# Rotation tables by one transpose of a narrow tile and row-repeating loads from a DRAM scratch, in a hybrid attention and gMLP block

## The chip, the cores and the metric

One core of a Trainium2 chip runs the whole kernel. The metric is the device time of one execution in microseconds (us), and a time given for a kernel is the median of several executions. The profile is of one execution; its span runs from the first instruction to the last.

Engines: PE is TensorE (matmuls and transposes by matmul), PEld its weight loads, DVE VectorE, ACT ScalarE, POOL GpSimd, and SP the engine whose queue issues most of this kernel's DMAs. PSUM is the memory into which PE accumulates; SBUF holds everything else on the chip; DRAM is the memory off the engines.

## The reference

One layer on a sequence of 1024 positions of width 1024, in float32. A root-mean-square norm is followed by one wide projection whose columns are queries, keys, values, gates and the inputs of a gMLP branch. What concerns the change is the rotation of the first 16 of the 64 dimensions of each query and key head:

```python
def partial_rope(x, pos):
    half = ROPE_DIM // 2          # 8
    inv_freq = ROPE_THETA ** (-(jnp.arange(half, dtype=jnp.float32) * 2.0) / ROPE_DIM)
    ang = pos.astype(jnp.float32)[:, None] * inv_freq[None, :]
    cos = jnp.cos(ang)[None, :, None, :]
    sin = jnp.sin(ang)[None, :, None, :]
    ...
    out = jnp.concatenate([x1 * cos - x2 * sin, x2 * cos + x1 * sin, rest], axis=-1)
```

The rotated queries and keys go into windowed attention with sinks (16 query heads, 2 key heads). Its output and the gMLP's are gated, projected, added to the residual and normed once more. The tables of cosines and sines depend on the position and on 8 frequencies alone, and are the same for all heads.

## The kernel before, in words

**Matmuls.** Every projection is a product of 1024x1024 blocks. `gemm_pair` takes two blocks of 128 output features (a pair, named by its first block m = 0, 2, 4, 6) and computes them by seven products instead of eight (b11, t1, t2, b21, t3, b22, t4, in this order), on sums and differences of quarters. A product (`product`, the matmul of L362) is 12 matmuls of 128x512: 4 steps of the inner dimension, each as high part by high part, high by low, and low by high. The high and low parts of a weight tile `wr` or of a sum of weight tiles `s` are `wh` (cast on ACT, L176) and `wl` (subtraction on DVE, L177).

**Around a pair.** Behind each product a hook is called; further work is put in there piece by piece, by generators that go on at each call. While a pair runs, the weight parts of the next one are made: its two tiles `wr` (four DMAs of 128 KB each for a query pair, L212, on SP) are loaded a pair earlier still, DVE forms their sums (L262 to L265), ACT and DVE split them. After t3, DVE subtracts the accumulator from x22 (L397); t4 accumulates into that same bank of PSUM, so t4 has to wait for L397. After b21, L392 adds to x11, and after b22, L401 to x12.

**Order.** Tiles have a fixed number of buffers per tag (`wr` 3, `wh` and `wl` 3 each, `rot` 5, `qhl` 3). A scheduler sets the order of each engine's instructions from the dependencies and its own estimate of durations; the engines then run their streams in that order, each instruction waiting for its semaphores. A DMA that waits at the head of SP's queue holds all behind it. SP's DMAs use eight semaphores in turn, so the ninth also waits for the first to have landed.

**The change's place.** The stage computes the queries, pairs m = 0, 2, 4, 6, through `gemm_pair(hb, finish, part_of_q)`. Each finished quarter goes to DRAM unrotated (`q_raw`, L520) and split into high and low parts (`q_hl`, L1241, from tiles `qhl` made by L1233 and L1236). At m = 2 the generator `rope_tables` makes two tables `tab`, of cosines and of sines, each 128x512: partition 64a + 8h + d holds frequency d for half a of the positions, the same for the eight h, and the 512 columns are the positions of that half. At m = 4 the generators `rotate_keys` and `rotate` begin: they load the rows to be rotated (`rot<-k_raw` L1254, `rot<-q_raw` L1290), multiply by the tables on DVE (L1271 to L1280 for the keys, L1310 to L1317 for the queries) and write the result over its place in `k_dr` and `q_hl`. A further `rotate` follows in the next pair, the first of `z` (destination `z_dr`), whose results only the second half of attention needs. The next pair after that begins attention: its score matmuls (L1438) read tiles `k` and `q` that SP loads from `k_dr` and `q_hl` (L1353, L1385).

**How the tables are made before.** The host passes cosines and sines as 128 x (8 tiles of positions x 16). Both are loaded into one tile. For each table DVE copies it, four times 128x128 (L1214), into a `wide` tile in which the frequencies stand eight times; PE transposes the four pieces (L1221) into a bank of tag `tp`; ACT copies the bank to `tab` (L1222).

## Time and profile before

| | |
|---|---|
| time, median of 3 runs | 897.91 us (896.01 to 897.95) |
| span of the profiled execution | 895.1 us |
| PE busy | 883.5 us, 99% of the span |
| DVE, ACT, POOL busy | 685.0, 580.7, 152.2 us |
| granted TensorE clock, mean | 0.998 |
| place of `rope_tables` in the span | 228 us (load of the tables) to 240 us (last copy to `tab`) |

The timed runs stand 0.9 to 2.9 us above the span of the profiled execution: the page counts only from the first instruction to the last. A busy PE is one in which matmuls follow each other; a matmul's own duration overlaps that of the next, so that a step between two starts (about 0.227 us in a product here) is what one costs, not its duration of 0.39 us.

### The profile page before, as it was taken

The numbers are of one execution on the slowest core, as the hardware profiler recorded it, in microseconds if no ns is written. First come the engines' busy times: TensorE is split into PE (matmuls) and PEld (weight loads), VectorE is DVE, ScalarE is ACT, GpSimd is POOL, SyncE is SP. The second block draws the span as 40 slices with busy tenths as digits, with TensorE's granted clock in tenths as the row PEclk, the third lists the DMA queues.
The fourth block names the chain that finished last, engine by engine and source line by source line (L and its number), as shares of the span: only waits on it lengthen the run. The fifth ranks groups of instructions, "written<-read, shape, count | busy, mean of one in ns | idle before, by whom it ended". The sixth has DMA issues, their size and how long they took to land.

```text
span 895.1 us, 13162 instructions
## 1 busy us (share of the span) xinstructions
PE 883.5 (99%) x4117; PEld 730.8 (82%) x4117; DVE 685.0 (77%) x1362; ACT 580.7 (65%) x1189; POOL 152.2 (17%) x218
## 2 busy tenths in 40 slices
PE   9999999999999999999999999999999999999997
PEld 6888888888888888888888888887888888888886
DVE  7879966566686778888878888846796588479886
ACT  6875523334445489999989999964685375467443
POOL 3322222203030011111211011101121121110012
PEclk9999999999999999999999999999999999999999
DMA  9998888858778767887776689989899789998523
GB/s 333 216 280 207 270 202 172 172 159 266 245 247 299 205 186 188 210 196 192 179 234 216 228 225 229 243 297 336 313 286 385 284 227 255 307 294 283 189 105 131
DMA packets 130962, 212.40 MB, mean 237 GB/s; under 512 B 12778, under 2 KB 59370, under 8 KB 130892
## 3 DMA queue, kind: packets, MB, share of 16 engines
q1 hardware_dynamic: 108280, 148.36, 49.9%
q0 software_dynamic: 22464, 62.93, 31.4%
q8 instruction: 33, 0.54, 0.2%
q14 instruction: 37, 0.30, 0.1%
q10 hardware_dynamic: 148, 0.27, 0.1%
HBM read 146.37 MB, written 86.11 MB: 260 GB/s over the span
## 4 chain that ended last, share of the span: by engine, by line
PE 90%; issue 3%; ACT 3%; DMA 2%; DVE 1%; SPq 0%; POOL 0%; ACTq 0%; POOLq 0%
PE ps_mm L362 39%; PE ps_o L362 25%; PE ps_tp L362 6%; PE ps_sc L362 3%; PE ps_o L793 3%; PE ps_tp L793 2%; PE ps_mm L793 2%; PE ps_sc L1438 2%; PE ps_tp L1511 2%; PE ps_tp L1109 2%; PE ps_o L1546 2%; PE ps_sc L793 1%; DMA a_dr<-x 1%; DMA wr<-in_x_dram 1%; PE ps_sc L663 1%
## 5 line engine op out<-in xcount | busy, mean ns | idle before, releaser
L176 ACT CAST wh<-s 128x1024 fp32r<-128x1024 f32 (+1 forms) x79 | 79.4, 1007 | 75.9 <-PE ps_mm L362 27.6
L177 DVE TENSOR_TENSOR wl<-wr,wh 128x512 fp32r<-128x512 f32 (+1 forms) x77 | 72.1, 938 | 60.0 <-ACT wh L176 59.1
L177 DVE TENSOR_TENSOR wl<-s,wh 128x1024 fp32r<-128x1024 f32 (+1 forms) x79 | 92.6, 1173 | 9.7 <-ACT wh L176 9.5
L176 ACT CAST wh<-wr 128x512 fp32r<-128x512 f32 (+1 forms) x77 | 63.0, 819 | 54.6 <-PE ps_mm L362 31.6
L362 PE MATMUL ps_o<-T_t1h,wh 128*128 128x512 f32 x148 | 57.8, 391 | 0.0
L362 PE MATMUL ps_o<-T_t1h,wl 128*128 128x512 f32 x148 | 57.7, 390 | 0.0
L362 PE MATMUL ps_o<-T_t1l,wh 128*128 128x512 f32 x148 | 57.6, 389 | 0.0
L362 PE MATMUL ps_mm<-T_t3h,wh 128*128 128x512 f32 x140 | 55.0, 393 | 2.0 <-ACT x L387 2.0
L1444 ACT COPY sl<-ps_sc 128x384 f32<-128x384 f32 (+2 forms) x128 | 51.8, 456 | 7.0 <-DVE sm L1450 7.0
L1466 ACT ACTIVATE pr<-pr,sm 128x192 f32<-128x192 f32 (+2 forms) x128 | 56.2, 443 | 0.1
L1450 DVE CUSTOM_DVE_ANT_0 pr<-sl,nsink_sb 128x192 f32<-128x192 f32 (+2 forms) x128 | 48.1, 400 | 10.0 <-ACT sl L1444 8.9
L362 PE MATMUL ps_mm<-T_b11h,wh 128*128 128x512 f32 x140 | 55.0, 393 | 0.0
L362 PE MATMUL ps_mm<-T_b11l,wh 128*128 128x512 f32 x140 | 54.6, 390 | 0.0
L362 PE MATMUL ps_mm<-T_t3h,wl 128*128 128x512 f32 x140 | 54.6, 390 | 0.0
L362 PE MATMUL ps_mm<-T_b11h,wl 128*128 128x512 f32 x140 | 54.6, 390 | 0.0
L362 PE MATMUL ps_mm<-T_t2l,wh 128*128 128x512 f32 x140 | 54.6, 390 | 0.0
L362 PE MATMUL ps_mm<-T_t3l,wh 128*128 128x512 f32 x140 | 54.6, 390 | 0.0
L362 PE MATMUL ps_mm<-T_t2h,wh 128*128 128x512 f32 x140 | 54.6, 390 | 0.0
L362 PE MATMUL ps_mm<-T_t2h,wl 128*128 128x512 f32 x140 | 54.5, 389 | 0.0
L362 PE MATMUL ps_mm<-T_t4h,wh 128*128 128x512 f32 x136 | 53.4, 393 | 0.0
L362 PE MATMUL ps_mm<-T_t4h,wl 128*128 128x512 f32 x136 | 53.1, 390 | 0.0
L362 PE MATMUL ps_mm<-T_t4l,wh 128*128 128x512 f32 x136 | 53.0, 389 | 0.0
(425 smaller groups left out, 2455.0 us busy)
## 6 DMA issues: line engine op xcount, KB each, us to landing
wr<-in_w_dram SPq DMA_DIRECT2D x86, 256.0 KB
sums<-in_w_dram POOLq DMA_DIRECT2D x20, 512.0 KB, 6.7
s<-sums SPq DMA_DIRECT2D x20, 512.0 KB
q_hl<-qhl SPq DMA_DIRECT2D x16, 512.0 KB
q<-q_hl SPq DMA_DIRECT2D x64, 128.0 KB
y_dr<-x POOLq DMA_DIRECT2D x28, 256.0 KB, 6.7
g<-in_w_dram POOLq DMA_DIRECT2D x12, 512.0 KB, 6.0
wr<-in_w_dram SPq DMA_DIRECT2D x11, 512.0 KB
```

The lines of the kernel that those rows point to most:

```text
L176: hi_of.append(nc.scalar.copy(hi, src))
L177: lo_of.append(nc.vector.tensor_sub(lo, src, hi.bitcast(F32)))
L362: nc.tensor.matmul(acc, lt, rt, start=fresh and k == 0 and n == 0, stop=k == 3 and n == 2, skip_group_check=True,)
L663: turns.append(nc.tensor.transpose(pt[:, i * P : (i + 1) * P], xt[:, k * P : (k + 1) * P], ident[:]))
L793: mm = nc.tensor.matmul(acc[:], lt, rt, start=fresh and k == 0 and n == 0, stop=stops and k == 3 and n == terms[-1], skip_group_check=True,)
L1109: nc.tensor.matmul(pm[:, t * P : (t + 1) * P], xh[:, half * 4 + t, g * P : (g + 1) * P], bias[-1][1][:, g % 4, :], start=True, stop=True,)
L1438: nc.tensor.matmul(sc, q_of[:, c, i * P : (i + 1) * P], kt[:, :, lo:hi], start=True, stop=True)
L1444: copies.append(nc.scalar.copy(two, sc))
L1450: nc.vector.tensor_tensor_reduce(v, two[:, 0, :], two[:, 1, :], 1.0, nsk[:, i : i + 1], op0=ALU.add, op1=ALU.min, accum_out=nmax[:, c, i : ...
L1466: e = nc.scalar.activation(v, v, AF.Exp, bias=nmax[:, c, i : i + 1], scale=-1.0, accum_out=sums[:, c, i : i + 1])
L1511: nc.tensor.transpose(dst, pr[:, i, block * P : block * P + width], ident[:])
L1546: nc.tensor.matmul(po[:, first], va[1][:, vs], a[:, n, first], start=n == 0, stop=n == 1, skip_group_check=True)
```

## The change

`rope_tables` loads the same two tables, and then makes one narrow tile of 128x128: 64 columns (8 tiles of positions by 8 frequencies) of cosines and 64 of sines, by two copies. One transpose turns it, so that a row is one frequency of one tile of positions. ACT copies the 128x128 to SBUF, and two DMAs on SP put it into a DRAM scratch `rope_dr` of 2 x 8 x 1024. Two hooks later each half of each table is loaded from there by a DMA on SP that reads the 8 rows eight times (four DMAs, 64 rows of 512 each). The eight wide copies, seven of the transposes and the two copies of 128x512 on ACT are gone. The number of yields is five in both. The order of all that follows on the engines is the scheduler's, made anew.

```diff
+    rope_dr = scratch("rope_dr", (2, 8, S))
...
-        for src in (both[:, 0, :, 0:8], both[:, 1, :, 8:16]):
-            tab = mtile([P, HALF], F32, f"tab{len(tables)}", 1, pool)
-            wide = rot_tile()
-            for i in range(4):
-                nc.vector.tensor_copy(
-                    wide[:, i * P : (i + 1) * P].rearrange("p (a h d) -> p a h d", a=2, h=8),
-                    src[:, i : i + 5 : 4, :].unsqueeze(2).broadcast_to([P, 2, 8, 8]),
+        narrow = rot_tile()[:, 0:P]
+        for f in range(2):
+            nc.vector.tensor_copy(
+                narrow[:, 64 * f : 64 * f + 64].rearrange("p (n d) -> p n d", n=NT),
+                both[:, f, :, 8 * f : 8 * f + 8],
+            )
+        yield
+        pt = bank("tp")
+        nc.tensor.transpose(pt[:, 0:P], narrow, ident[:])
+        rows = rot_tile()[:, 0:P]
+        nc.scalar.copy(rows, pt[:, 0:P])
+        for f in range(2):
+            nc.sync.dma_start(rope_dr[f].rearrange("d (n p) -> n d p", n=NT), rows[64 * f : 64 * f + 64])
+        yield
+        yield
+        for f in range(2):
+            tab = mtile([P, HALF], F32, f"tab{f}", 1, pool)
+            for half in range(2):
+                nc.sync.dma_start(
+                    tab[64 * half : 64 * half + 64],
+                    rope_dr[f][:, half_of(half)].unsqueeze(0).broadcast_to([8, 8, HALF]),
                 )
-            yield
-            pt = bank("tp")
-            for i in range(4):
-                nc.tensor.transpose(pt[:, i * P : (i + 1) * P], wide[:, i * P : (i + 1) * P], ident[:])
-            nc.scalar.copy(tab[:], pt[:])
             tables.append(tab)
-            yield
+        yield
```

Lines of the changed kernel stand 1 lower up to the change (L362 is L363 there) and 10 lower behind it (L1236 is L1246).

**SP in pair m = 2, before.** The weight tiles of pair m = 6 are wr_2227 and wr_2228; the keys' rows are loaded as soon as `k_raw` stands.

```order
L1254 DMA rot_2256<-k_raw 16x1x512 x2
L212 DMA wr_2227<-in_w_dram 128x2x128 x4
L1254 DMA rot_2257<-k_raw 16x1x512
L520 DMA q_raw<-x_2060 128x512
L212 DMA wr_2228<-in_w_dram 128x2x128 x2
L1241 DMA q_hl<-qhl_2136 128x2x512
L520 DMA q_raw<-x_2062 128x512
L1241 DMA q_hl<-qhl_2165 128x2x512
L520 DMA q_raw<-x_2061 128x512
L212 DMA wr_2228<-in_w_dram 128x2x128 x2
L1254 DMA rot_2257<-k_raw 16x1x512
```

The same stretch after the change, up to the loads of the keys' rows; here the weight tiles of pair m = 6 are wr_2219 and wr_2220, and qhl_2210 is the last split quarter of pair m = 2.

```order
L1223 DMA rope_dr<-rot_2115 8x8x128 x2
L213 DMA wr_2219<-in_w_dram 128x2x128 x3
L1229 DMA tab_329_2162<-rope_dr 64x1x512
L521 DMA q_raw<-x_2061 128x512
...
L1251 DMA q_hl<-qhl_2157 128x2x512
L1229 DMA tab_330_2165<-rope_dr 64x1x512 x2
...
L1251 DMA q_hl<-qhl_2210 128x2x512
L213 DMA wr_2219<-in_w_dram 128x2x128
L213 DMA wr_2220<-in_w_dram 128x2x128 x4
L1264 DMA rot_2248<-k_raw 16x1x512 x2
L1264 DMA rot_2249<-k_raw 16x1x512 x2
```

The last five of the eight weight loads, and all loads of the keys' rows, have moved behind the last split quarter of pair m = 2.

**DVE in pair m = 4, before.** x_2240 and x_2242 are x11 and x22 of this pair, rot the keys' rows, wl_2332 the first low part of pair m = 6 (whose sums s_2237 and s_2238 are made further up).

```order
L177 TENSOR_TENSOR wl_2296<-wr_2048,wh_2295 128x512
L392 TENSOR_TENSOR x_2240<-x_2240,ps_o_2311 128x512
L1277 TENSOR_TENSOR rot_2257<-rot_2257,tab_319_2092 128x512
L177 TENSOR_TENSOR wl_2332<-wr_2227,wh_2331 128x1024
L1236 SCALAR_TENSOR_TENSOR qhl_2326<-x_2240,qhl_2326 128x256 x2
L1278 TENSOR_TENSOR rot_2256<-rot_2256,tab_328_2145 128x512
L397 TENSOR_TENSOR x_2242<-x_2242,ps_mm_2239 128x512
```

The same stretch after the change, where x22 is x_2234 and its instruction is L398.

```order
L178 TENSOR_TENSOR wl_2288<-wr_2049,wh_2287 128x512
L263 TENSOR_TENSOR s_2229<-wr_2220 128x512
L265 TENSOR_TENSOR s_2230<-wr_2219,wr_2220 128x512
L264 TENSOR_TENSOR s_2229<-s_2229,wr_2219 128x512
L1281 TENSOR_TENSOR rot_2250<-rot_2248,tab_329_2162 128x512
L393 TENSOR_TENSOR x_2232<-x_2232,ps_o_2303 128x512
L178 TENSOR_TENSOR wl_2324<-wr_2219,wh_2323 128x1024
L1282 TENSOR_TENSOR rot_2251<-rot_2249,tab_330_2165 128x512
L1288 TENSOR_TENSOR rot_2248<-rot_2248,tab_330_2165 128x512
L1284 TENSOR_TENSOR rot_2250<-rot_2250,rot_2251 128x512
L1287 TENSOR_TENSOR rot_2249<-rot_2249,tab_329_2162 128x512
L398 TENSOR_TENSOR x_2234<-x_2234,ps_mm_2231 128x512
```

Three of the sums of pair m = 6 and four more rotations now stand between `wl` and the subtraction from x22. On PE the order differs in one further place, here: the first three matmuls of b11 of pair m = 6 have moved in front of t4 of pair m = 4.

**SP from the first `z` pair to the second step of attention, before.** wr_2768 and wr_2769 are weight tiles, qhl_2708 and qhl_2741 the last rotated queries, q_2842 the queries of attention's third step (the first of its second block of positions).

```order
L212 DMA wr_2768<-in_w_dram 128x512
L520 DMA z_dr<-x_2610 128x512
L212 DMA wr_2768<-in_w_dram 128x512
L212 DMA wr_2769<-in_w_dram 128x512 x2
L1241 DMA q_hl<-qhl_2708 8x8x512 x4
L1241 DMA q_hl<-qhl_2741 8x8x512 x4
L520 DMA z_dr<-x_2761 128x512
L1385 DMA q_2842<-q_hl 64x4x128 x2
```

After the change, where the tiles are wr_2760 and wr_2761, qhl_2700 and qhl_2733, k_2832 and q_2834:

```order
L521 DMA z_dr<-x_2602 128x512
L521 DMA z_dr<-x_2753 128x512
L213 DMA wr_2760<-in_w_dram 128x512 x2
L1251 DMA q_hl<-qhl_2700 8x8x512 x4
L1251 DMA q_hl<-qhl_2733 8x8x512 x4
L213 DMA wr_2761<-in_w_dram 128x512 x2
L1363 DMA k_2832<-k_dr 128x2x256
L1395 DMA q_2834<-q_hl 64x4x128 x2
```

The second weight tile and the tile k of attention's third step have moved behind the eight stores of rotated queries (k_2840 stood much further up before), and the queries of that step come last.

## The prediction

> **What bounds the kernel now.** I read the page first: the span, the engines' busy time, and the chain that ended last.
>
> ```profile
> span 895.1 us, 13162 instructions
> PE 883.5 (99%) x4117; PEld 730.8 (82%) x4117; DVE 685.0 (77%) x1362; ACT 580.7 (65%) x1189; POOL 152.2 (17%) x218
> PE 90%; issue 3%; ACT 3%; DMA 2%; DVE 1%; SPq 0%; POOL 0%; ACTq 0%; POOLq 0%
> ```
>
> PE is busy but for 11.6 us, and is 90% of the chain. So a matmul taken away shortens the kernel by its step, and work on another engine costs nothing until PE waits for it. All else turns on whether PE keeps its matmuls back to back. Next the chain, restricted to pair m = 2 of the queries, where the tables are made (columns: start, us, what).
>
> ```profile
> 224.11 2.95 PE ps_mm L362 x13
> 227.06 2.72 PE ps_o L362 x12
> 229.78 2.73 PE ps_mm L362 x12
> 232.51 0.68 PE ps_tp L1221 x4
> 233.19 2.76 PE ps_o L362 x12
> 235.94 2.72 PE ps_mm L362 x12
> 238.67 0.44 PE ps_tp L1221 x4
> 239.10 2.77 PE ps_o L362 x12
> 241.88 2.49 PE ps_mm L362 x11
> ```
>
> Twelve matmuls take 2.72 us, with nothing between the products but the two groups of four transposes (the last row is cut by the window at 244.37). A measurement of this kernel can tell about 0.3% from no change, 2.7 us; the place concerned holds less than that.
>
> **Transposes.** They cost 0.68 and 0.44 us, and the products behind them 2.76 and 2.77 instead of 2.72: in all 0.68 + 0.04 + 0.44 + 0.05 = 1.21 us. The second group is 0.11 us per transpose. The first is 0.24 us longer: PE reached it when DVE had only begun the copies.
>
> ```profile
> L1214 DVE COPY rot<-rot x8: 219/220/222, 232.2 to 233.1; 128x128 f32<-128x128 f32 x8
> L1221 PE MATMUL ps_tp<-ident,rot x8: 270/276/303, 232.5 to 238.8; 128*128 128x128 f32 x8
> L1222 ACT COPY tab<-ps_tp x2: 586/590/594, 233.3 to 239.1; 128x512 f32<-128x512 f32 x2
> ```
>
> The single transpose stays at the first place and still waits for two copies: 0.24 + 0.11 + 0.04 = 0.39 us. The gain is 1.21 - 0.39 = 0.82 us. Bounds: 1.21 if the one transpose costs nothing, 0.49 if the first place costs as much as now. I take 0.82, since the wait there is for copies that start at the same time in both kernels.
>
> The trace lists each transpose with 276 ns, but the step between two in a row is 0.11 us, and the sum goes by the step. The Trainium skill, "TensorE: Matmul & The Clock Gate", section "Part 4: PE-mode transpose", gives about 275 ns for a 128x128 transpose inside a kernel, most of it access latency; the trace's duration agrees (276 ns), its step does not. By the page's figure seven would be worth 1.9 us; this is a rival below.
>
> **Copies.** On DVE eight copies of 220 ns go and two narrower ones come, at most 220 ns each: about 1.3 us less. On ACT two copies of 590 ns go and one of a quarter of the size comes. Neither engine is on the chain here, so I count both at nothing; PE hides them, as it hid the more.
>
> **New DMAs.** SP gets two stores and four loads more. The nearest rows are small loads by it and the weight loads around them.
>
> ```profile
> 226.15 0.56 SPq L212 DMA_DIRECT2D wr<-in_w_dram  x1
> 231.54 1.47 SPq L1254 DMA_DIRECT2D rot<-k_raw  x2
> 233.97 2.57 SPq L212 DMA_DIRECT2D wr<-in_w_dram  x4
> 247.59 0.37 SPq L1241 DMA_DIRECT2D q_hl<-qhl  x1
> 287.97 0.51 SPq L212 DMA_DIRECT2D wr<-in_w_dram  x1
> 229.63 0.69 DVE L262 TENSOR_TENSOR s<-wr 128x512 f32<-128x512 f32 x1 [2.38 <-DMA wr<-in_w_dram]
> 293.64 0.69 DVE L262 TENSOR_TENSOR s<-wr 128x512 f32<-128x512 f32 x1 [1.65 <-DMA wr<-in_w_dram]
> ```
>
> An issue takes about 0.65 us (2.57 for four), six take 3.9 us. From issue to landing there are two measured cases, in which DVE stood waiting for a weight tile: issue at 226.15, DVE on at 229.63, so 3.5 us; and 287.97 to 293.64, 5.7 us. These are my two bounds for every landing below. The new stores are issued when ACT has copied the rows, about 233.9 by the 233.3 at which L1222 starts now. They land at 237.4 to 239.6; the first table load reaches the head of SP's queue behind three weight loads at 233.9 + 1.3 + 1.9 = 237.1. It holds the queue for 0.3 to 2.5 us. Behind it are a `q_raw` store and split quarters, for which no engine waits soon, and the last of them (the `q_hl` store that is at 247.59 now) is set by DVE, not by SP. So the wait itself I count at nothing. The tables are there before 248, and the first rotation that uses them now stands far behind.
>
> **What has moved behind them.** This is where the change can cost. Five of the weight loads of pair m = 6 now follow that `q_hl` store. Everything in this pair comes 0.82 earlier, so it is issued at 246.8 and done at 247.1; the last weight load is the fifth behind it, issued at 247.1 + 4 x 0.64 = 249.7. It lands at 253.2 (3.5) or 255.4 (5.7). On DVE the sums that need it stand ahead of the subtraction from x22, which t4 of pair m = 4 waits for:
>
> ```profile
> 253.22 0.69 DVE L177 TENSOR_TENSOR wl<-wr,wh 128x512 fp32r<-128x512 f32 x1 [1.34 <-ACT wh L176]
> 255.51 0.69 DVE L392 TENSOR_TENSOR x<-x,ps_o 128x512 f32<-128x512 f32 x1 [1.60 <-PE ps_o L362]
> 256.12 0.68 DVE L1277 TENSOR_TENSOR rot<-rot,tab 128x512 f32<-128x512 f32 x1
> 256.72 1.22 DVE L177 TENSOR_TENSOR wl<-wr,wh 128x1024 fp32r<-128x1024 f32 x1
> 257.86 0.76 DVE L1236 SCALAR_TENSOR_TENSOR qhl<-x,qhl 128x256 fp32r<-128x256 f32 x2
> 259.13 0.68 DVE L397 TENSOR_TENSOR x<-x,ps_mm 128x512 f32<-128x512 f32 x1
> 260.75 0.39 PE L362 MATMUL ps_mm<-T_t4h,wh 128*128 128x512 f32 x1
> ```
>
> Now L397 ends at 259.8 and t4 starts at 260.75: about 0.9 us of cover. By these starts a 128x512 operation takes 0.60 us of DVE's stream (255.51 to 256.12) and the 128x1024 one 1.14. After the change, from the landing on, there come ahead of the subtraction three sums, a rotation, the addition to x11, `wl` and four more rotations: nine small ones and a wide one, 9 x 0.60 + 1.14 = 6.5 us, then its own 0.7. With the landing at 253.2 it ends at 260.4. t4 would be due at 260.75 - 0.82 + 3 x 0.227 = 260.6, the three b11 matmuls being moved in front of it. So PE waits for nothing with the early landing, by 0.2 us, and 2.0 us with the late one (262.6). I take the early one, since SP has little ahead of these loads (in the late case a 512 KB store had been issued 0.4 us before, in this one 2.9 us before). With a cover so thin I put 0.2 us of wait into the sum.
>
> The Trainium skill, "DMA: Bandwidth & Descriptors", section "Anatomy of one DMA — SWDGE (gpsimd) path", gives about 2.0 us fixed per transfer and a rate of 436 GB/s, for GpSimd's queue: an estimate of 2.3 us for 128 KB, by which the last load would land at 252.0 and DVE would not be held by it at all. The trace has 3.5 us and 5.7 us for loads of this queue, and those are used.
>
> **Pair z and attention.** The stores of rotated queries now stand ahead of a weight tile and of the k and q tiles of attention's third step.
>
> ```profile
> 303.23 5.42 SPq L1241 DMA_DIRECT2D q_hl<-qhl  x8
> 309.44 1.64 SPq L1385 DMA_DIRECT2D q<-q_hl  x2
> 311.60 0.80 SPq L212 DMA_DIRECT2D wr<-in_w_dram  x2
> 319.42 0.52 PE L1438 MATMUL ps_sc<-k,q 128*128 128x384 f32 x2
> 305.52 0.42 ACT L1444 COPY sl<-ps_sc 128x128 f32<-128x128 f32 x2
> ```
>
> ACT now casts the rotated queries behind the copies of the first scores (305.5 now, so about 304.7 to 305.5), the eight stores go out from 305.6 to 311.0, two weight loads until 311.8, k until 312.4 and q until 313.7, its second issue at 313.0. It lands at 316.5 to 318.7; the scores are due at 319.42 - 0.82 = 318.6. So 0 to 0.1 us of wait: nothing.
>
> **Sum.** -0.82 + 0.2 + 0 = -0.6 us: the profiled 895.1 us would be 894.5. I carry the same difference to the median of the runs, which stands 2.8 us above that span: 897.3 us.
>
> **Rivals.**
> 1. *Forecast, no change that can be told (0.88).* The gain is real and smaller than 2.7 us. For it: 1.21 us is all that the transposes cost, and the waits I find are within 2 us.
> 2. *The weight loads come late and PE waits (0.08), slower.* Mechanism: the queue that the table loads hold pushes the last weight load of pair m = 6, and the sum that waits for it stands ahead of L398 on DVE. It decides from a landing at 253.4 on; each us later is one us of PE. With 5.7 us it is 2.0, net +1.2 us (899.1), still within 0.3%. It is slower by over 0.3% from a landing at 253.4 + 0.8 + 2.7 = 256.9, or when another load of the moved order adds as much: say +3.5 us, 901.4. Against it: both measured landings are shorter.
> 3. *Each transpose is worth its whole duration.* 7 x 0.276 = 1.9 us, 896.0. Against it: two groups of four took 0.68 and 0.44 us. I give it 0.05 of the 0.88, since it too is within 0.3%.
> 4. *DVE's and ACT's relief lets PE close gaps elsewhere (0.04), faster.* Over 2.7 us would have to come out of the 11.6 us in which PE is not busy, and in these pairs it is busy throughout. It takes a luckier order in attention, say -3.2 us, 894.7.
>
> **Numbers.** Predicted 897.3 us. The range is from 896.0 (transposes at full duration) to 899.3 (late landing, 899.1, and the 0.1 of attention): below lies the 0.04 of rival 4, above the 0.08 of rival 2, the rest is room for other runs. Faster 0.04, same 0.88, slower 0.08.
>
> **What would show it.** Right: one transpose at 232.5 and no gap at 238.5; pair m = 4 beginning 0.8 us earlier than now (244.4); L263 on the last weight tile at about 253.2, L398 ending near 260.4, and t4 of pair m = 4 behind three b11 matmuls with at most a few tenths of idle PE. Wrong: PE idle by over 1 us before t4 with L398 as the releaser, or before the scores at 318.6 with a DMA as the releaser; or a span that differs by over 2.7 us with PE back to back in these pairs, which would put the cause where I did not look.

## The result, and the profile after

The changed kernel took 899.7 us (median of 7 runs, 898.88 to 903.11), the kernel before 897.73 us (median of 7 beside it): ratio 1.0043, 95% interval 1.0032 to 1.0054. The forecast was 897.3 us and no change, with a range to 899.3. On another chip the changed kernel came out at 1.0057 (1.0036 to 1.0077), so it is slower. The quotient of the two medians is 1.0022 on the first chip and 1.0055 on the other, so the size of the loss is known no better than as 0.2 to 0.6 per cent; in all the experiments below that quotient lies within 0.001 of the ratio given. The profiled execution of the changed kernel took 899.36 us, with a span of 897.4 us (before: 895.1).

The page after, to be held against the first lines of the prediction:

```profile
span 897.4 us, 13147 instructions
PE 884.4 (99%) x4110; PEld 729.9 (81%) x4110; DVE 684.4 (76%) x1356; ACT 579.6 (65%) x1188; POOL 152.0 (17%) x218
PE 81%; DMA 5%; DVE 4%; ACT 4%; issue 4%; SPq 1%; POOL 0%; ACTq 0%; DVEq 0%; POOLq 0%
```

PE's own work hardly moved, but its share of the chain fell from 90% to 81%, and DMA and DVE took that place: PE now waits. The chain of pair m = 2 after the change (start, us, what):

```profile
229.64 2.73 PE ps_mm L363 x12
232.37 0.17 issue
232.54 0.30 PE ps_tp L1219
232.84 2.74 PE ps_o L363 x12
235.58 2.72 PE ps_mm L363 x12
238.30 2.72 PE ps_o L363 x12
241.02 3.17 PE ps_mm L363 x14
```

From the product at 229.64 to the one at 241.02 there are 11.38 us, where the kernel before had 12.10 (229.78 to 241.88). The transposes gave 0.72 us. The rest of the story is behind 244 us. Busy time in the stretch from there to the third step of attention (length, then busy us of PE, PEld, DVE, ACT and POOL, granted clock, DMA share, GB/s), before:

```profile
244.00:330.00 86.00, 86.00 (x391) 71.61 (x390) 65.24 (x140) 48.07 (x103) 9.85 (x17) 1.00 0.77 242
```

and after:

```profile
244.00:330.00 86.00, 82.84 (x367) 67.11 (x366) 62.47 (x127) 43.66 (x90) 8.93 (x16) 1.00 0.75 234
```

PE, never idle here before, is idle for 3.16 us. PE's timeline after the change tells where (start, duration, instruction, and in brackets the idle time before it and what ended it):

```profile
260.93 0.50 PE L363 MATMUL ps_mm<-T_t4h,wh 128*128 128x512 f32 x1 [0.19 <-DVE x L398]
...
281.30 0.50 PE L363 MATMUL ps_mm<-T_t4h,wh 128*128 128x512 f32 x1 [1.67 <-DVE x L398]
281.64 0.40 PE L363 MATMUL ps_mm<-T_t4l,wh 128*128 128x512 f32 x1
...
301.50 0.50 PE L363 MATMUL ps_mm<-T_t4h,wh 128*128 128x512 f32 x1 [0.83 <-DVE x L398]
...
322.89 0.59 PE L1448 MATMUL ps_sc<-k,q 128*128 128x384 f32 x2 [0.46 <-DMA q<-q_hl]
```

The four waits make 3.15 of the 3.16 us. Three products t4 wait for the subtraction from x22, and one pair of score matmuls waits for its queries. A wait costs more than the brackets say: they count from the modelled end of the last matmul, 0.16 us behind its step, and the step behind the pause is longer too (281.30 to 281.64 is 0.34 us instead of 0.23). In starts of the same work (of the chain's pieces, as shown above, in the first two rows, of the first matmul in the others) the changed kernel stands against the kernel before as follows.

| matmul | before | after | lag |
|---|---|---|---|
| product ahead of the first transposes | 229.78 | 229.64 | -0.14 |
| t4 of m = 2, behind them | 241.88 | 241.02 | -0.86 |
| t4 of m = 4 | 260.75 | 260.93 | +0.18 |
| t4 of m = 6 | 279.79 | 281.30 | +1.51 |
| t4 of the first z pair | 298.83 | 301.50 | +2.67 |
| scores of attention's third step | 319.42 | 322.89 | +3.47 |
| t3 of a later pair, behind ACT's L388 | 613.52 | 615.80 | +2.28 |

Three b11 matmuls (3 x 0.227 = 0.68 us) stand ahead of t4 of m = 4 now, so 0.68 of the step from -0.86 to +0.18 is an exchange and only the rest, 0.36 us, a loss. The last row gives 1.8 us back: there the kernel before waited in this profile (2.01 us), the changed one, coming 4.1 us late by then, hardly (0.18 us).

Why DVE is late is in its timeline after the change:

```profile
253.64 0.69 DVE L263 TENSOR_TENSOR s<-wr 128x512 f32<-128x512 f32 x1 [0.58 <-DMA wr<-in_w_dram]
...
260.20 0.68 DVE L398 TENSOR_TENSOR x<-x,ps_mm 128x512 f32<-128x512 f32 x1
...
273.27 0.69 DVE L263 TENSOR_TENSOR s<-wr 128x512 f32<-128x512 f32 x1 [1.67 <-DMA wr<-in_w_dram]
...
280.56 0.68 DVE L398 TENSOR_TENSOR x<-x,ps_mm 128x512 f32<-128x512 f32 x1
...
300.16 0.69 DVE L263 TENSOR_TENSOR s<-wr 128x512 f32<-128x512 f32 x1 [2.80 <-DMA wr<-in_w_dram]
300.77 0.68 DVE L398 TENSOR_TENSOR x<-x,ps_mm 128x512 f32<-128x512 f32 x1
```

Each time DVE stands at the first sum of weight tiles until the last of them has landed, and the subtraction comes behind it in the same stream. In pair m = 6 the kernel before made that sum at 268.67 without a wait. SP's timeline after tells when the loads went out:

```profile
236.94 0.64 SPq L1229 DMA_DIRECT2D tab<-rope_dr  x1
...
241.00 2.29 SPq L1229 DMA_DIRECT2D tab<-rope_dr  x2
...
247.14 3.38 SPq L213 DMA_DIRECT2D wr<-in_w_dram  x5
...
264.05 2.95 SPq L521 DMA_DIRECT2D q_raw<-x  x2
267.09 2.49 SPq L213 DMA_DIRECT2D wr<-in_w_dram  x2
...
309.51 5.14 SPq L1251 DMA_DIRECT2D q_hl<-qhl  x8
314.70 1.39 SPq L213 DMA_DIRECT2D wr<-in_w_dram  x2
316.13 0.50 SPq L1363 DMA_DIRECT2D k<-k_dr  x1
316.74 1.29 SPq L1395 DMA_DIRECT2D q<-q_hl  x2
```

and the same queue before, for the pair behind m = 6:

```profile
257.97 0.33 SPq L212 DMA_DIRECT2D wr<-in_w_dram  x1
...
260.22 0.45 SPq L212 DMA_DIRECT2D wr<-in_w_dram  x1
```

The two loads that went out at 257.97 and 260.22 now stand behind the last split quarters and two `q_raw` stores, and go out from 267.09 on. SP has to wait for the sources of these stores (the first goes out at 264.05, when the addition L402 that makes its source has ended at 264.02), and the two issues take 2.95 us.

### The profile page after: what moved, and what is told of

Same layout as the page of the kernel before. It is cut to its first block, busy times and chain, and to the rows that moved or that the text cites. A ratio compares the mean times of both kernels' runs of the same rounds, so it can differ in the third digit from the quotient of the medians.

```text
span 897.4 us, 13147 instructions
## 1 busy us (share of the span) xinstructions
PE 884.4 (99%) x4110; PEld 729.9 (81%) x4110; DVE 684.4 (76%) x1356; ACT 579.6 (65%) x1188; POOL 152.0 (17%) x218
## 4 chain that ended last, share of the span: by engine, by line
PE 81%; DMA 5%; DVE 4%; ACT 4%; issue 4%; SPq 1%; POOL 0%; ACTq 0%; DVEq 0%; POOLq 0%
PE ps_mm L363 35%; PE ps_o L363 21%; PE ps_tp L363 6%; PE ps_sc L363 3%; PE ps_tp L794 2%; PE ps_o L794 2%; PE ps_mm L794 2%; PE ps_sc L1448 2%; PE ps_tp L1521 2%; PE ps_tp L1110 2%; DMA wr<-in_w_dram 2%; PE ps_o L1556 1%; DMA q_hl<-qhl 1%; PE ps_sc L794 1%; DMA a_dr<-x 1%
## 5 line engine op out<-in xcount | busy, mean ns | idle before, releaser
L363 PE MATMUL ps_o<-T_t1h,wh 128*128 128x512 f32 x148 | 57.9, 391 | 0.0
L363 PE MATMUL ps_o<-T_t1h,wl 128*128 128x512 f32 x148 | 57.7, 390 | 0.0
L363 PE MATMUL ps_o<-T_t1l,wh 128*128 128x512 f32 x148 | 57.6, 389 | 0.0
L363 PE MATMUL ps_mm<-T_t4h,wh 128*128 128x512 f32 x136 | 54.0, 397 | 2.7 <-DVE x L398 2.7
L363 PE MATMUL ps_mm<-T_t3h,wh 128*128 128x512 f32 x140 | 55.0, 393 | 0.2 <-ACT x L388 0.2
L363 PE MATMUL ps_mm<-T_b11h,wh 128*128 128x512 f32 x140 | 55.0, 393 | 0.0
L363 PE MATMUL ps_mm<-T_b11l,wh 128*128 128x512 f32 x140 | 54.6, 390 | 0.0
L363 PE MATMUL ps_mm<-T_t3h,wl 128*128 128x512 f32 x140 | 54.6, 390 | 0.0
L363 PE MATMUL ps_mm<-T_b11h,wl 128*128 128x512 f32 x140 | 54.6, 390 | 0.0
L363 PE MATMUL ps_mm<-T_t2l,wh 128*128 128x512 f32 x140 | 54.6, 390 | 0.0
L363 PE MATMUL ps_mm<-T_t2h,wh 128*128 128x512 f32 x140 | 54.6, 390 | 0.0
L363 PE MATMUL ps_mm<-T_t3l,wh 128*128 128x512 f32 x140 | 54.6, 390 | 0.0
L363 PE MATMUL ps_mm<-T_t2h,wl 128*128 128x512 f32 x140 | 54.5, 389 | 0.0
L363 PE MATMUL ps_mm<-T_t4h,wl 128*128 128x512 f32 x136 | 53.1, 391 | 0.0
L363 PE MATMUL ps_mm<-T_t4l,wh 128*128 128x512 f32 x136 | 53.1, 390 | 0.0
```

Of the source, the lines that this page charges most:

```text
L363: nc.tensor.matmul(acc, lt, rt, start=fresh and k == 0 and n == 0, stop=k == 3 and n == 2, skip_group_check=True,)
```

## The experiments

Theories. **The late loads:** the change gains its 0.7 us, but the scheduler, which has to place six DMAs and a table that is ready later, lets loads fall behind stores on SP (why it places them so was not looked into); DVE, ACT and PE, each in the order of its stream, run into them. **The traffic:** the new DMAs move 0.6 MB through the same DMA engines, and this slows the loads beside them. **The held queue:** a table load waits at the head of SP's queue for its store to land and holds the weight loads. All ratios below are to the kernel before on the same chip.

**1. Transposes alone.** The kernel before with one transpose per table and no new DMA.

```diff
-            for i in range(4):
-                nc.tensor.transpose(pt[:, i * P : (i + 1) * P], wide[:, i * P : (i + 1) * P], ident[:])
-            nc.scalar.copy(tab[:], pt[:])
+            nc.tensor.transpose(pt[:, 0:P], wide[:, 0:P], ident[:])
+            nc.scalar.copy(
+                tab[:].rearrange("p (i n) -> p i n", i=4), pt[:, 0:P].unsqueeze(1).broadcast_to([P, 4, P])
+            )
```

> The kernel before with one transpose per table instead of four; ACT writes the one 128x128 piece four times over into the table, so three quarters of each table hold the wrong positions. No DMA is added, and the tables are never in DRAM. The theory of the order (the matmuls gained are 0.7 us, and the loss comes from weight loads that the scheduler puts behind the stores of split quarters, with the sums that need them ahead of the subtraction from x22 on DVE): PE order is that of before less six transposes, 6 x 0.11 = 0.7 us and some waiting at the first transpose gained; in pairs m = 4 and m = 6 the weight loads stand early, so no wait there; in the first z pair all four loads stand behind the last split quarter and one sum stands ahead of the subtraction, so up to 1 us of PE waiting before t4; ratio 0.999 to 1.001. The theory of the traffic and that of the held queue (the loss comes from the new DMAs themselves): none are there, so ratio 0.9992 and no wait at any t4.

Measured: 1.0002 (0.9991 to 1.0012). From t2 to t4 of pair m = 2 PE took 11.24 us instead of 12.10 and so gained 0.86 us; it waited 0.39 us before t4 of m = 6, not in the z pair as I had thought, and stood 1.36 us near 613. Such a gain is too small to be seen, and even an edit that adds no DMA re-orders the streams enough to give part of it back.

**2. Late loads alone.** The kernel before, with weight loads (`late`: all behind the first three of pair m = 6, behind the first two of the next pairs) put off until the pair that runs when they would go out has issued its last store:

```diff
...
+        while late:
+            after(nc.sync.dma_start(*late.pop(0)), q_stores[-1])
```

> The kernel before, its rotation tables untouched, computing the same; only the last weight loads of three pairs are issued behind the last split quarter of the pair before, as the change's order has them: five of eight for pair m = 6, two of four for each of the first two z pairs. PE's order is that of before, and on DVE the sums that need these loads stand ahead of the subtraction from x22. The theory of the order: DVE stands waiting for wr ahead of the first sum, and PE for the subtraction before t4 in pair m = 6 (about 1 to 2 us, the loads issued 10 us later than now and landing near 274 to 276 in the span) and up to 0.5 us in pair m = 4; ratio 1.001 to 1.003, with part of it given back where PE stands waiting 2.0 us near 613 now. The theories of the traffic and of the table load that holds the queue: no table goes through DRAM here, so no t4 waits and the ratio is 1.000.

Measured: 1.0038 (1.0026 to 1.0050). PE's order is that of before and no table is in DRAM, and a loss like the change's is there. On DVE the sums that need these loads have moved too, as the data come late. From the timeline of this kernel (L269 is the first sum, L409 the subtraction; DVE and PE):

```profile
274.19 0.69 DVE L269 TENSOR_TENSOR s<-wr 128x512 f32<-128x512 f32 x1 [1.93 <-DMA wr<-in_w_dram]
...
279.62 0.68 DVE L409 TENSOR_TENSOR x<-x,ps_mm 128x512 f32<-128x512 f32 x1
280.35 0.50 PE L374 MATMUL ps_mm<-T_t4h,wh 128*128 128x512 f32 x1 [1.09 <-DVE x L409]
```

This is what the changed kernel shows at 273 to 281 us. The first z pair waits as well (0.63 us), pair m = 4 does not. These 1.72 us need not be the whole of its loss: near 613 PE, 2.0 us late by then, still waits 2.47 us in this profile. The last of the five loads of pair m = 6, issued at 250.0 (247.32 + 3.38 - 0.65), let DVE go on at 253.47; in the changed kernel, with the table loads before it, 249.9 and 253.64. So the load landed after 3.4 and 3.8 us; the new traffic makes 0.35 us of that at most.

**3. Sums behind the subtraction.** The changed kernel, late loads and all; the sums of pairs m = 6 and of two z pairs are tied behind the subtraction of the pair that runs.

```diff
-            make_sums(term_of_x11[0] if done[0] <= 4 else None)
+            make_sums(term_of_x11[0] if done[0] <= 4 else of_x22[0] if done[0] in (8, 9, 10) else None)
...
```

> The changed kernel, its six table DMAs and its late weight loads left as they are, computing the same; the sums of weight tiles are tied behind the subtraction from x22 in pairs m = 4, m = 6 and the first z pair. The theory of the order: the three waits for the subtraction before t4 (0.2, 1.7 and 0.8 us in the changed kernel's trace, 0.5 + 2.0 + 1.2 = 3.6 us of PE's lag on the kernel before) go, the wait for q in attention (about 1 us) stays; up to 613 us PE then lags the kernel before by 0.5 us instead of 4.1. Of this 1.8 us was given back near 613 anyway, so the end gains 2 to 3 us on the changed kernel: ratio to before 0.999 to 1.001. The theories of the traffic and of the held queue: the DMAs are the same, the late data reach PE later by the same amount through the weight parts instead of the subtraction: ratio as after the change, 1.003 to 1.005.

Measured: 1.0072 (1.0051 to 1.0092), no better than the change itself, by interval not told apart from it; the number that I had expected is refuted. The waits of PE in this kernel, 244 to 330 us (waiting line, releaser, us in all, times, longest):

```profile
PE ps_o L364 <- ACT wh L177: 2.3, 1, 2.3
PE ps_sc L1449 <- DMA q<-q_hl: 1.2, 1, 1.2
PE ps_mm L364 <- ACT x L389: 0.3, 1, 0.3
PE ps_o L364 <- DVE wl L178: 0.2, 1, 0.2
PE ps_sc L1449 <- ACT sl L1455: 0.2, 1, 0.2
```

No t4 waits any more; t1 of pair m = 6 waits for its weight part instead. So it is not the order of two instructions on DVE that costs, but that the data come late: whoever is made to meet them later passes the lateness on. Why they come late this run does not tell: this path through the weight parts is what I had written down for the traffic and the held queue.

**4. Tables on POOL's queue.** The six DMAs as `nc.gpsimd.dma_start`, nothing else changed.

> The changed kernel with its two stores and four table loads issued by POOL instead of SP, computing the same; same traffic, through the same DRAM scratch. The scheduler's order on PE is then that of before less the seven transposes; on SP four of eight weight loads of pair m = 6 and all but one of the others stand early again, the last of them still behind the last split quarter; on DVE the sums stand ahead of the subtraction by 6 to 11 rows. The theory of the order: the waits before t4 shrink to under 0.5 us each: ratio 0.999 to 1.001. The theory of the held queue: the same, since SP is free of the table loads. The theory of the traffic: 0.55 MB more go over the same DMA engines at the same time, so the weight tiles land as late as after the change: ratio 1.003 to 1.005.

Measured: 1.0032 (1.0019 to 1.0045). SP is free of the tables and nothing is gained that can be told (the intervals overlap), so the held queue is not the chief cause; a share of it stays possible by this run alone. By its ratio alone the theory of the traffic would fit, but the trace has the last weight load of pair m = 6 still issued late (248.6), DVE idle for 4.1 us at 252.22 until it can make the first sum, and 1.03 and 0.45 us of PE before two t4's, where I had expected under 0.5 each, with 0.73 us more for an ACT copy.

**5. Rows from the host.** The host lays out the tables as 8 rows of 1024, and the four row-repeating loads read them from the inputs: `rope_dr = (cos, sin)`, without copies, transpose and stores.

> The changed kernel with the tables passed in by the host already laid out as 8 rows of 1024 positions, so that the four row-repeating loads read them straight from the inputs, at the start of pair m = 2: no copy, no transpose and no store is left, the loads are the same 0.5 MB; it computes the same. The order on SP is then nearly that of before: six of the eight weight loads of pair m = 6 and the keys' rows stand where they stood, the last two ahead of the last two split quarters. The theory of the late loads (what costs time is that weight loads go out late and the engines behind them run dry, whoever causes it): PE loses the 1.2 us of the transposes and no t4 of pairs m = 4 and m = 6 waits by over 0.3 us; up to 1 us may be lost in the first z pair, whose last two loads stand behind the last split quarter, and 1 us in attention; ratio 0.998 to 1.000. The theory of the traffic (the repeated rows' 0.5 MB slow the loads beside them): the loads are still there, weight tiles land later than before; ratio 1.002 or more.

Measured: 1.0024 (1.0012 to 1.0037), against my 0.998 to 1.000. Pair m = 4 does not wait, as its loads stand early; pairs m = 6 and z wait 0.55 and 0.86 us, the latter since DVE stood 3.58 us for loads behind the last split quarter. Repeated rows are still loaded here, so this run cannot part traffic from order; runs 11 and 12 go further.

**6. Loads first.** The changed kernel, with the weight loads of pairs m = 6 and z put ahead of the last quarter's stores of pairs m = 2 and m = 4 (`split_next`, which issues them, also goes ahead of that quarter's `finish`).

```diff
...
-            put(q_raw, m + i, half, q[:])
+            store = put(q_raw, m + i, half, q[:])
+            if sign < 0 and m in (2, 4):
+                for move in loads_of[done[0] + 1]:
+                    after(store, move)
```

> The changed kernel, computing the same, with one thing put back: the weight loads of pairs m = 6 and of the first z pair are tied ahead of the last quarter's stores of pairs m = 2 and m = 4, as they stood in the kernel before. Tables, scratch and their six DMAs on SP are as after the change. The theory of the late loads: issued by 247 and 261 us instead of 250 and 269, they land by 250.5 and 265; the waits for the subtraction before t4 of pairs m = 4 and m = 6 (0.2 and 1.7 us after the change) shrink to under 0.4 each, that of the z pair (0.8) and of attention's q (0.5) stay; PE stands 2 us ahead of the changed kernel in attention, of which 1 us is left at the end; ratio to before 1.000 to 1.003. The theory of the traffic: the same DMAs at the same places, ratio 1.003 to 1.005 as after the change.

Measured: 1.0020 (1.0007 to 1.0034). PE's waits from 244 to 330 us in this kernel:

```profile
PE ps_sc L1457 <- DMA q<-q_hl: 0.8, 1, 0.8
PE ps_mm L365 <- DVE x L400: 0.4, 1, 0.4
```

t4 waits 0.4 us in all instead of 2.7 and the wait for q stays, as expected; the wait of the z pair, which I had expected to stay, has gone as well. The table loads go out within 0.7 us of where they did after the change (237.38 to 243.72).

**7. Tables later.** Three more `yield` ahead of the four table loads of the changed kernel.

> The changed kernel, computing the same, with the four table loads three hooks later, at the first hook of pair m = 4, and the keys' rotation one hook later for it. On SP six of the eight weight loads of pair m = 6 then stand ahead of the last two split quarters, and those of the first z pair nearly as before. The theory of the late loads: last loads issued near 248 land near 251.5, t4 of pair m = 4 waits for up to 0.8 us; t4 of pair m = 6 does not wait by over 0.4; ratio 0.999 to 1.002. The theory of the traffic: 1.003 to 1.005 as after the change.

Measured: 1.0017 (1.0004 to 1.0030). One t4 waits, 0.41 us, at m = 4. Moved to where fewer loads are pushed, the same DMAs go with a loss of less than half, by the ratios (0.0017 against 0.0043).

**8. Tables a pair earlier.** `if m == 0` instead of `if m == 2` for `rope_tables`.

> The changed kernel, computing the same, with the whole making of the tables moved from pair m = 2 to pair m = 0, 37 us earlier, so that no table load stands near the weight loads of pair m = 6. Yet the scheduler puts four of these eight behind the last split quarter of pair m = 2 again. The theory of the late loads: the waits before t4 of pairs m = 4 and m = 6 come back (together 1 to 3 us) with the tables long there; ratio 1.001 to 1.004. The theory of the traffic and that of the table load that holds the queue: nothing of the tables is left near pairs m = 4 and m = 6, so no wait there; ratio 0.999 to 1.000.

Measured: 1.0028 (1.0017 to 1.0039). No table load is near, and PE waits all the same: 0.55 us for a weight part `wl` of m = 6, 0.55 and 0.18 before t4 of m = 6 and z. That is 1.3 us, against both rivals; that t4 of m = 4 would wait, as I had expected of the late loads, did not come.

**9 and 10. Both kernels again.**

> The kernel before, unchanged, against itself: ratio 1.000, its interval shows what a ratio here can tell. Its new profile tells whether the 2.0 us that PE waits near 613 us for ACT's copy (held by the store a_dr) is the same each time: all theories expect 1 to 2 us there and nothing before any t4 of the queries.

> The changed kernel, unchanged, on the chip of the other experiments. All theories: ratio 1.003 to 1.005. The theory of the late loads: waits for the subtraction before t4 of pairs m = 4, m = 6 and of the first z pair and for q in attention within 0.5 us of those of the first profile (0.2, 1.7, 0.8 and 0.5), since they follow from the order of the streams; under 0.5 us near 613, where PE comes late.

Measured: 0.9997 (0.9988 to 1.0006) for the kernel before against itself, and 1.0057 (1.0036 to 1.0077) for the changed one. The t4 waits of the changed kernel come back (0.60, 1.33 and 0.24 us, the last a little further off than the 0.5 us that I had allowed), and PE waits 0.84 us at t3 of the later pair instead of under 0.5. But the wait for q, 0.46 us in the first profile, is 2.73 here, and more comes with it. PE's timeline in this second profile:

```profile
324.85 0.98 PE L1448 MATMUL ps_sc<-k,q 128*128 128x384 f32 x2 [2.73 <-DMA q<-q_hl]
325.63 0.63 PE L363 MATMUL ps_mm<-T_t4h,wh 128*128 128x512 f32 x1
326.05 0.63 PE L363 MATMUL ps_mm<-T_t4l,wh 128*128 128x512 f32 x1
326.48 0.63 PE L363 MATMUL ps_mm<-T_t4h,wl 128*128 128x512 f32 x1
```

The matmuls follow each other by 0.43 us instead of 0.23. The stretches of the same profile show why; the number behind POOL's busy time is the granted clock:

```profile
322.00:324.80 2.80, 0.12 (x1) 0.00 (x0) 2.31 (x4) 0.32 (x1) 0.00 (x0) 0.99 0.82 198
324.80:326.00 1.20, 1.15 (x3) 1.14 (x4) 1.17 (x4) 1.18 (x3) 0.00 (x0) 0.50 0.25 82
326.00:328.00 2.00, 2.00 (x6) 1.56 (x5) 1.97 (x3) 1.18 (x6) 0.00 (x0) 0.50 0.71 205
328.00:332.00 4.00, 4.00 (x19) 3.31 (x19) 2.37 (x9) 2.47 (x6) 0.00 (x0) 0.98 0.92 293
```

After the pause the clock is at 0.50 for about 3.2 us, which costs about 1.6 us more. The other thing that these two runs tell is how much of the 1.8 us given back near 613 was luck. The kernel before in its first profile:

```profile
613.52 0.50 PE L362 MATMUL ps_mm<-T_t3h,wh 128*128 128x512 f32 x1 [2.01 <-ACT x L387]
```

and in the second:

```profile
612.71 0.50 PE L362 MATMUL ps_mm<-T_t3h,wh 128*128 128x512 f32 x1 [0.76 <-ACT x L387]
```

So before waits there for 0.8 to 2.0 us, for an ACT copy that itself waits until the store `a_dr` lands. It is a place where some of any gain or loss ahead of it is lost, and not a fixed amount.

**11. Both put back.** The changed kernel with the edits of runs 6 and 7 together; all its DMAs are kept.

> The changed kernel, computing the same, with both of the partial remedies: table loads three hooks later and the weight loads tied ahead of the last quarter's stores of pairs m = 2 and m = 4. All six table DMAs and the scratch are kept. The theory of the late loads: all eight weight loads of pair m = 6 are issued by 247 us, DVE does not stand waiting for one by over 2 us, no t4 of the queries waits by over 0.3 us, PE stands 1 us ahead of the kernel before at 300 us; 0 to 1 us of that is lost near 613, where PE then waits the longer for the store a_dr; ratio 0.998 to 1.001, and if PE's wait there goes over 2 us the clock may fall for some us and cost 2 more in some executions. The theory of the traffic: same DMAs, ratio 1.003 to 1.005.

Measured: 1.0005 (0.9996 to 1.0014). PE's waits from 244 to 330 us in this kernel:

```profile
PE ps_mm L365 <- DVE x L400: 0.6, 1, 0.6
```

The same table through the same scratch with the same six DMAs on SP, and what is left of the loss is too small to be told; PE's order is that of before less the seven transposes. One of the four table loads goes out at 237.74 and three at 246.97, right behind the last weight loads of pair m = 6 (244.13 to 245.74), so the traffic still stands beside them; in run 6 all four stay where the change put them, and the t4 waits fell to 0.4 us. With run 2, which has the loss without them, this decides against the traffic and the held queue as the chief cause. One t4 still waits 0.6 us, where I had expected under 0.3. The profiled execution, 892.8 us of span, is the shortest of its runs; the median does not keep that.

**12. Host rows, three pairs.** Run 5 with the loads of pairs m = 6 and of both z pairs tied ahead.

> The tables read straight from host rows of 8 x 1024 as in the run with rows from the host (no copy, transpose or store), and the weight loads of pairs m = 6 and of both z pairs tied ahead of the last quarter's stores (three of four in the last); it computes the same. The theory of the late loads: the 3.6 us for which DVE stood at the first z pair in that run go down to under 2, the wait before its t4 (0.9) to under 0.3; PE 1.2 us ahead of the kernel before at 300 us; ratio 0.998 to 1.001, better than that run's 1.0024. The theory of the traffic: 0.5 MB of row-repeating loads as there, ratio 1.002 again.

Measured: 1.0010 (0.9997 to 1.0023): lower than run 5 with the same row-repeating loads, as the late loads have it, though the intervals overlap, and not by the waits that I named. DVE stood longer at the z pair (5.45 us), which no longer held t4 there; PE waited 0.58 us at t4 of m = 6 and 0.68 us for an ACT copy.

**13 to 15. The wait for the queries.** To take away the wait for q, the rotation of the second half is begun ahead of attention's first loads: alone (13), with the loads first (14), and with everything (15).

```diff
-    steps_of_q += [first_loads(), rotate(1, 1)]
+    steps_of_q += [rotate(1, 0), first_loads()]
```

> The changed kernel, computing the same, with one thing moved: in the first z pair the rotation of the second half of the query heads is begun ahead of the first loads of attention instead of behind them, so that its eight stores go out some 6 us earlier and the queries of attention's third step are loaded in time. The late weight loads of the queries' pairs are left. The theory that the wait for these queries (0.5 us in one profile of the changed kernel, 2.7 us and a fall of the granted clock to 0.50 in the other) is the chief part of the loss: no such wait, ratio 1.000 to 1.002. The theory that the late weight loads are the chief part: the waits before t4 of pairs m = 4, m = 6 and z stay (2 to 3 us together), ratio 1.002 to 1.004.

> The changed kernel, computing the same, with the weight loads tied ahead of the last quarter's stores (as in the run that put the loads first, 1.0020) and with the second half's rotation begun earlier. Both theories of the late loads, that of weights and that of attention's queries: no wait before t4 over 0.4 us and none for q: 0.8 to 1.5 us better than the loads alone, ratio 0.9995 to 1.0015. The theory of the traffic: 1.003 or more.

> The changed kernel, computing the same, with all remedies: table loads three hooks later, weight loads of pairs m = 6 and of both z pairs tied ahead of the last quarter's stores, second half's rotation earlier. If the change's own gain of 0.8 us of matmuls can be had at all, it is had here: PE 1 us ahead of the kernel before at 300 us and at 600, ratio 0.998 to 1.000. If the wait for the store a_dr near 613 swallows what PE is ahead: 0.9995 to 1.001.

Measured: 1.0073 (1.0053 to 1.0092), 1.0063 (1.0041 to 1.0085) and 1.0047 (1.0033 to 1.0061). All three miss. By itself the edit did not do what it was for: PE's waits from 244 to 330 us in run 13,

```profile
PE ps_mm L363 <- DVE x L398: 3.1, 3, 1.4
PE ps_sc L1448 <- ACT sl L1454: 1.3, 1, 1.3
PE ps_sc L1448 <- DMA q<-q_hl: 1.2, 1, 1.2
```

have the wait for q still there, and a new one at the first scores, whose loads now go out later. In run 14 the wait for q is gone, but PE waits 1.82 us for an ACT copy of the first scores, and the granted clock falls to 0.50 behind it. In run 15, where hardly any t4 waits, the queries alone hold PE:

```profile
322.89 0.60 PE L1460 MATMUL ps_sc<-k,q 128*128 128x384 f32 x2 [2.65 <-DMA q<-q_hl]
```

There the eight stores went out from 304.13 instead of 309.51 and q's second issue at 315.14 instead of 317.4, but the load took 7.75 us to land. So this wait can by itself be as dear as those before t4. Which share each has in the unprofiled runs of the changed kernel stays open: no run took away the wait for q alone.

**All together.** PE's idle time from 244 to 330 us (86.00 less its busy time) in each kernel's one profile, against its ratio:

| kernel | idle, us | ratio |
|---|---|---|
| before again (9) | 0.00 | 0.9997 |
| transposes alone (1) | 0.39 | 1.0002 |
| tables later (7) | 0.50 | 1.0017 |
| both put back (11) | 0.63 | 1.0005 |
| host rows, three pairs (12) | 1.29 | 1.0010 |
| loads first (6) | 1.34 | 1.0020 |
| a pair earlier (8) | 1.43 | 1.0028 |
| host rows (5) | 1.46 | 1.0024 |
| late loads alone (2) | 1.72 | 1.0038 |
| loads and rotation first (14) | 2.23 | 1.0063 |
| POOL's queue (4) | 2.35 | 1.0032 |
| all and rotation first (15) | 2.99 | 1.0047 |
| after (first, and again 10) | 3.16, 4.91 | 1.0043, 1.0057 |
| sums behind (3) | 4.27 | 1.0072 |
| rotation first (13) | 5.62 | 1.0073 |

In the main the time follows this idle time, whoever is waited for, and not the number of DMAs or transposes. Neighbouring rows do not keep the order, as each idle time is of one execution; what the lowered clock costs in the profiles of runs 14 and 10 is not in it. No version beats the kernel before by what can be told.

## Why the prediction was wrong, point by point

- **Transposes, -0.82:** right but for 0.1 us, -0.72 measured. The one that is left costs 0.17 + 0.30 + 0.02 = 0.49 us instead of 0.39. That steps count and not durations was right: with seven whole durations, as the figure of the Trainium skill has them ("TensorE: Matmul & The Clock Gate", section "Part 4: PE-mode transpose"), the products behind would have come another 1.2 us earlier.
- **Copies, nothing:** right for ACT's copy. The transpose starts 0.20 us after the second narrow copy has ended (232.34 to 232.54) and 0.57 us after the last matmul, where the second group of the kernel before started after 0.24 (238.27 to 238.51): that fits the wait for two copies that the transposes' sum has in it, which came out 0.1 us longer.
- **New DMAs at nothing:** right for their own hold. The first table load goes out at 236.94 (forecast 237.1) in 0.64 us; the last two hold the queue for about 1 us longer than two issues, at 241.00 to 243.29, and no engine waits for that.
- **Weight loads of m = 6, +0.2 us at t4 of m = 4:** right in mechanism, and in part lucky in size. Landing 253.6 (forecast 253.2), L398 done at 260.88 (260.4), 0.19 us of idle PE. The walk itself gave no wait (L398 done 0.2 us before t4 was due); the 0.2 was put in as a margin, and in starts the loss is 0.36 us. The last load, issued at 249.9, landed after 3.7 us. The estimate of 2.3 us from the Trainium skill, "DMA: Bandwidth & Descriptors", section "Anatomy of one DMA — SWDGE (gpsimd) path", would have had it there at 252.2. That estimate is for GpSimd's queue; this load on SP's queue does not agree with it.
- **The sum, -0.82 + 0.2 + 0: this is the step that failed.** It took a wait found in one pair for all that the moved order could do, and rested on "the waits I find are within 2 us" for the rest. The same walk, from the issue of the loads over DVE's stream to t4, was not made for pair m = 6 and the first z pair, whose loads had moved behind stores as well. There the run shows 1.67 and 0.83 us of idle PE, worth 2.0 and 1.2 us of lag by the table (the 0.68 of the exchange taken off the row of t4 of m = 4).
- **Pair z and attention, nothing: wrong too.** The eight stores were to go out from 305.6 and q's second issue at 313.0; they went at 309.51 and 317.4, because the rotations on DVE, which feed them, stood behind the sums that waited for weights until 300.16. Landing took 5.5 us in this profile, within my bounds of 3.5 to 5.7, but 7.1 in the second (317.7 to 324.85). Those bounds were taken from loads of weights.
- **Rivals:** the second one was the nearest. It had the late weight loads and DVE's sums ahead of L398, but pair m = 4 as the place and the queue held by the table loads as the cause; the measured 899.7 us lies between its 899.1 and its 901.4 ("or when another load of the moved order adds as much"). It got 0.08 because the landings measured before were short. The clause that another load might be late was the likely case, as loads of three pairs had moved. Both signs that were named as "wrong" came: idle PE by over 1 us before t4 with L398 as the releaser (1.67 us, at m = 6), and a wait for scores with a DMA as the releaser (0.46 us in the first profile, 2.73 in the second).

## What to carry to other kernels

Where a scheduler makes the order anew, the cost of an edit is not only at the edit: list every load that has moved behind a store, for all the stages in which the order differs, and walk each to the engine that meets it, before a sum is made. With the bound engine at 99%, the saving of 0.7 us was worth less here than the order that it disturbed; compare such a change with the order tied to what it was (run 11) before judging it. Moving the consumer of late data did not help (run 3); moving the load did (run 6).

## What the runs showed of the hardware

- **The clock falls after pauses of about 2 us, and not always.** PE idle for 2.73 us (run 10), 2.47, 2.04 and 2.03 us (runs 2, 5 and 13, near 613 to 621) and even 1.82 us (run 14, at 307) was followed by a granted clock of 0.50 over some microseconds; after 2.01 us (before, first profile), 2.31 us (run 3, at 268) and 2.65 us (run 15, at 323) it stayed at 1.00. So in this range the length of a pause does not decide alone. The Trainium skill, "TensorE: Matmul & The Clock Gate", section "Part 1: The HAM clock gate (the "warmup" mystery)", puts the half rate behind an idle window of about 3.4 us that runs freely. That pauses of like length do and do not trip it agrees with a free-running window; that 1.82 us sufficed does not agree with its length. What else decides was not tried.
- **A load's landing on one queue spans 3.4 to 7.75 us:** 3.4 us for the last of five weight loads in run 2, 5.8 us for a single weight load in the changed kernel (issued at 294.36, DVE on at 300.16), 7.1 and 7.75 us for the queries in runs 10 and 15.
